# Issuing the loads of an average-pooling kernel from GpSimd's queue instead of SyncE's

## Chip, cores, metric

One core of one Trainium2 chip. The metric is the device time of one execution in microseconds (us), lower is better. A run's span in its profile is about 2 us shorter than its time.

## The reference

A 2x2 average pooling with stride 2 over a float32 tensor of 32x128x256x256. It reads 1074 MB and writes 268 MB; there are three additions and one multiplication for each output element.

```python
def reference(x, kernel_size, stride):          # 2, 2
    ...
    for i in range(h_out):
        for j in range(w_out):
            window = x[:, :, 2*i : 2*i + 2, 2*j : 2*j + 2]   # indices shortened
            output[:, :, i, j] = np.mean(window, axis=(2, 3))
```

## The kernel before

An output row needs two input rows, which lie one after the other in DRAM: 512 floats, 2 KiB, here called a row pair. A full tile holds 32 row pairs in each of 128 partitions. The layout "(p g)" gives each partition 32 row pairs that are adjacent in DRAM, so a load of 8 MiB is 128 pieces of 64 KiB, and a store of 2 MiB is 128 pieces of 16 KiB. There are two input buffers. The last two tiles are split into ten smaller parts, down to one row pair in each partition.

```python
sbuf = ctx.enter_context(tc.tile_pool(name="sbuf", bufs=2))
inv = 1.0 / float(k * k)
r0 = 0
for parts in plan:                       # [32] x 126, then [16, 8, 8], [8, 8, 8, 4, 2, 1, 1]
    in_tile = sbuf.tile([P, G_MAIN, s * w], mybir.dt.float32, name="in_tile")
    g0 = 0
    for g in parts:
        rows = P * g
        xt = xv[r0 : r0 + rows].rearrange("(p g) f -> p g f", p=P)
        ot = ov[r0 : r0 + rows].rearrange("(p g) f -> p g f", p=P)
        # ... r0 += rows
        it = in_tile[:, g0 : g0 + g]
        # ... g0 += g
        nc.sync.dma_start(out=it, in_=xt)                    # load, SyncE's queue
        nc.vector.tensor_add(out=it[:, :, 0:w], ...)         # upper row + lower row
        col_sum = sbuf.tile([P, G_MAIN, w_out], ..., bufs=3)
        nc.vector.tensor_add(out=col_sum[:, :g], ...)        # even columns + odd columns
        nc.scalar.mul(out=col_sum[:, :g], in_=col_sum[:, :g], mul=inv)
        nc.scalar.dma_start(out=ot, in_=col_sum[:, :g])      # store, ScalarE's queue
```

The load of tile i+2 goes into the buffer of tile i, so it may be issued when the second addition of tile i has read that buffer.

Of the kernel before, what the change touches and what calls it, by code (L numbers as in the profile page):

```python
# [1 line left out]

# [4 lines left out]


@with_exitstack  # L10
def kernel(
    ctx: ExitStack,
    tc: tile.TileContext,
    x: bass.AP,
    kernel_size: bass.AP,
    stride: bass.AP,
    out: bass.AP,
):
    nc = tc.nc
    P = nc.NUM_PARTITIONS  # L20

    n, c, h, w = x.shape
    k = int(kernel_size)
    s = int(stride)
    h_out = (h - k) // s + 1
    w_out = (w - k) // s + 1
    R = n * c * h_out

    if k == s and 2 <= k <= 4 and R > 0 and R % P == 0:
        _nonoverlap_pool(ctx, tc, x, out, k, n, c, h, w, h_out, w_out)  # L30
    else:
        _generic_pool(ctx, tc, x, out, k, s, n, c, h, w, h_out, w_out)


def _nonoverlap_pool(ctx, tc, x, out, k, n, c, h, w, h_out, w_out):
    nc = tc.nc
    P = nc.NUM_PARTITIONS
    s = k
    R = n * c * h_out

    hv = h_out * s
    xs = x if hv == h else x[:, :, 0:hv, :]
    xv = xs.rearrange("n c (ho a) w -> (n c ho) (a w)", a=s)
    ov = out.rearrange("n c ho wo -> (n c ho) wo")
    assert xv.shape == (R, s * w) and ov.shape == (R, w_out)

    wu = w_out * s

    unit_bytes = s * w * 4
    G_MAIN = max(1, min(R // P, (64 * 1024) // unit_bytes))  # L50

    total_units = R // P
    nmain, rem_units = divmod(total_units, G_MAIN)
    plan: list[list[int]] = [[G_MAIN] for _ in range(nmain)]
    if rem_units:
        plan.append([rem_units])

    if G_MAIN % 32 == 0 and nmain >= 4 and rem_units == 0:
        u = G_MAIN // 32
        tail = [  # L60
            [16 * u, 8 * u, 8 * u],
            [8 * u, 8 * u, 8 * u, 4 * u, 2 * u, u, u],
        ]
        assert all(sum(t) == G_MAIN for t in tail)
        plan = plan[:-2] + tail
# [6 lines that stand above are left out]
    for parts in plan:  # L72
# [6 lines that stand above are left out]
            r0 += rows  # L79

            it = in_tile[:, g0 : g0 + g]
            g0 += g

            nc.sync.dma_start(out=it, in_=xt)

            for di in range(1, k):
                nc.vector.tensor_add(  # L87
                    out=it[:, :, 0:w],
                    in0=it[:, :, 0:w],
                    in1=it[:, :, di * w : (di + 1) * w],  # L90
                )

            col_sum = sbuf.tile(
                [P, G_MAIN, w_out], mybir.dt.float32, name="col_sum", bufs=3
            )
            nc.vector.tensor_add(  # L96
                out=col_sum[:, :g],
                in0=it[:, :, 0:wu:s],
                in1=it[:, :, 1 : wu + 1 : s],
            )  # L100
            for dj in range(2, k):
                nc.vector.tensor_add(
                    out=col_sum[:, :g],
                    in0=col_sum[:, :g],
                    in1=it[:, :, dj : wu + dj : s],
                )

            nc.scalar.mul(out=col_sum[:, :g], in_=col_sum[:, :g], mul=inv)  # L108

            nc.scalar.dma_start(out=ot, in_=col_sum[:, :g])  # L110
        assert g0 <= G_MAIN

    assert r0 == R, (r0, R)


def _generic_pool(ctx, tc, x, out, k, s, n, c, h, w, h_out, w_out):
    nc = tc.nc
    P = nc.NUM_PARTITIONS

    planes = n * c  # L120
    xp = x.rearrange("n c h w -> (n c) h w")
    op = out.rearrange("n c ho wo -> (n c) ho wo")

    if h_out <= 0 or w_out <= 0 or planes == 0:
        return

    max_in_bytes_per_part = 48 * 1024

    def rows_for(bi):
        return (bi - 1) * s + k  # L130

    BI = 1
    while BI < h_out and rows_for(BI + 1) * w * 4 <= max_in_bytes_per_part:
        BI += 1

    inv = 1.0 / float(k * k)

    pool = ctx.enter_context(tc.tile_pool(name="gen", bufs=2))

    for p0 in range(0, planes, P):  # L140
        pn = min(P, planes - p0)
        for i0 in range(0, h_out, BI):
            bi = min(BI, h_out - i0)
            rows_needed = rows_for(bi)

            in_t = pool.tile([P, rows_for(BI), w], mybir.dt.float32, name="g_in")
            nc.sync.dma_start(
                out=in_t[:pn, :rows_needed, :],
                in_=xp[p0 : p0 + pn, i0 * s : i0 * s + rows_needed, :],
            )  # L150

            acc = pool.tile([P, BI, w_out], mybir.dt.float32, name="g_acc")
            first = True
            for di in range(k):
                for dj in range(k):
                    src = in_t[
                        :pn,
                        di : di + (bi - 1) * s + 1 : s,
                        dj : dj + (w_out - 1) * s + 1 : s,
                    ]  # L160
                    if first:
                        nc.vector.tensor_copy(out=acc[:pn, :bi, :], in_=src)
                        first = False
                    else:
                        nc.vector.tensor_add(
                            out=acc[:pn, :bi, :], in0=acc[:pn, :bi, :], in1=src
                        )

            nc.scalar.mul(out=acc[:pn, :bi, :], in_=acc[:pn, :bi, :], mul=inv)

            nc.scalar.dma_start(
                out=op[p0 : p0 + pn, i0 : i0 + bi, :], in_=acc[:pn, :bi, :]
            )


# [1 line left out]
_INS = ['x', 'kernel_size', 'stride']  # L177
_OUTS = [((32, 128, 128, 128), 'float32')]
#: Inputs that are plain numbers.
_NUMBERS = {'kernel_size': 2, 'stride': 2}  # L180


# [26 lines left out]
```

## Time and profile before

| | before |
|---|---|
| time, median of 2 runs | 3106.58 us (3106.37 to 3106.79) |
| DMA engines' time taken by packets, loads and stores | 79.8% and 20.2% |
| VectorE, ScalarE busy | 54%, 15% |
| one 64 KiB load packet, one 16 KiB store packet | 2.418 us, 0.611 us |
| a full tile's two additions | 8.69 + 4.43 us |

The first lines are from the page of the kernel before: the DMA rows of its 40 slices, and the queue part. A queue's line has its number, its kind, packets, megabytes, and the time its packets took as a share of 16 engines over the span.

```profile
DMA  9999999999999999999999999999999999999999
GB/s 418 436 439 425 436 439 425 436 438 429 433 439 430 431 439 434 427 439 435 426 438 436 427 437 436 428 436 437 427 436 437 428 436 437 429 435 437 432 431 396
...
q1 hardware_dynamic: 19584, 1073.75, 79.8%
q10 hardware_dynamic: 19584, 268.44, 20.2%
```

Queue q1 is the loads', q10 the stores'. Together their packets take 100% of the engines' time: the kernel is bound by the DMA engines, and there is no room in which a faster issue could show.

The view by windows of the kernel before (stretch in us, its length, busy time of each engine, granted clock, DMA share, GB/s) shows where the engines are not full: at the start and in the last 48 us.

```profile
0.00:24.00 24.00, 1.30 (x1) 1.28 (x1) 0.20 (x4) 1.00 0.93 393
24.00:3010.00 2986.00, 1625.35 (x248) 446.62 (x124) 0.00 (x0) 1.00 1.00 434
3010.00:3057.00 47.00, 26.24 (x4) 5.88 (x3) 0.00 (x0) 1.00 0.99 426
3057.00:3105.00 48.00, 28.50 (x20) 11.99 (x11) 0.00 (x0) 1.00 0.89 375
```

A stretch of the timeline of the kernel before (start, duration, engine, line, operation, and in brackets the idle time just before and what ended it). One row of it merges several issues of SyncE's queue:

```profile
1494.01 8.69 DVE L87 TENSOR_TENSOR in_tile<-in_tile 128x8192 f32<-128x8192 f32 x1 [10.97 <-DMA in_tile<-in_x_dram]
1502.79 4.42 DVE L96 TENSOR_TENSOR col_sum<-in_tile 128x4096 f32<-128x4096 f32 x1
1507.24 73.85 SPq L84 DMA_DIRECT2D in_tile<-in_x_dram  x4
1507.25 3.62 ACT L108 ACTIVATE col_sum<-col_sum 128x4096 f32<-128x4096 f32 x1 [20.56 <-DVE col_sum L96]
1510.89 0.34 ACTq L110 DMA_DIRECT2D out_dram<-col_sum  x1
1518.19 8.69 DVE L87 TENSOR_TENSOR in_tile<-in_tile 128x8192 f32<-128x8192 f32 x1 [10.97 <-DMA in_tile<-in_x_dram]
```

VectorE finishes tile i at 1507.21 and then waits 10.97 us for tile i+1 to land. The load of tile i+2 is issued at 1507.24, while tile i+1 is still arriving. Those 11 us are roughly the time by which a load is issued ahead of when the engines run out of loads: the slack.

The issues by size have the median time from issue to landing at the end of the line:

```profile
out_dram<-col_sum ACTq DMA_DIRECT2D x126, 2048.0 KB, 31.6
...
in_tile<-in_x_dram SPq DMA_DIRECT2D x126, 35.1
```

Last, the waits of SyncE's queue in the end of the kernel, from 3010 us on (sum, times, longest):

```profile
SPq L84 <- DVE col_sum L96: 26.4, 2, 13.2
SPq L84 <- DMA in_tile<-in_x_dram: 25.4, 3, 10.6
SPq L84 <- DMA out_dram<-col_sum: 23.7, 4, 15.3
```

Some of the last small loads wait for stores to land, though they share no data. Loads and stores draw their completion semaphores (the counters by which a finished transfer is reported) from one set of eight in this trace, and a load that gets a semaphore whose store is under way has to wait for it.

### The profile page before, as it was taken

The page shows a single profiled execution, that of the slowest core. Times are in us where ns is not written, and L with a number is a line of the kernel's source. Part 1 is how long each engine was busy: PE and PEld are TensorE (multiplying, and loading weights), DVE is VectorE, ACT ScalarE, POOL GpSimd, SP SyncE. Part 2 cuts the span into 40 slices and gives each one's busy share as a digit, 9 for nine tenths or more (in the row PEclk, how much of TensorE's full clock was granted, in tenths as well). Part 3 has the DMA queues.
Part 4 walks back from the last instruction along what each step waited for, and adds up shares of the span by engine and source line. Part 5 has one row for each costly group of instructions (what it writes and reads, how often), then busy time and mean ns, then how long its engine had stood idle before and what let it go on. Part 6 is the DMA issues. An engine that isn't in the chain of part 4 may idle for free. (4 is left out here: it accounts for less than half of the span.)

```text
span 3104.8 us, 1126 instructions
## 1 busy us (share of the span) xinstructions
DVE 1681.4 (54%) x272; ACT 465.8 (15%) x137; POOL 0.2 (0%) x4
## 2 busy tenths in 40 slices
DVE  4555555555555555555555555555555555555556
ACT  1111111111111111111111111111111111111112
POOL 0000000000000000000000000000000000000000
DMA  9999999999999999999999999999999999999999
GB/s 418 436 439 425 436 439 425 436 438 429 433 439 430 431 439 434 427 439 435 426 438 436 427 437 436 428 436 437 427 436 437 428 436 437 429 435 437 432 431 396
DMA packets 39176, 1342.26 MB, mean 432 GB/s; under 512 B 4352, under 2 KB 4736, under 8 KB 5888
## 3 DMA queue, kind: packets, MB, share of 16 engines
q1 hardware_dynamic: 19584, 1073.75, 79.8%
q10 hardware_dynamic: 19584, 268.44, 20.2%
q14 instruction: 8, 0.07, 0.0%
HBM read 1073.74 MB, written 268.44 MB: 432 GB/s over the span
## 5 line engine op out<-in xcount | busy, mean ns | idle before, releaser
L87 DVE TENSOR_TENSOR in_tile<-in_tile 128x8192 f32<-128x8192 f32 (+4 forms) x136 | 1113.9, 8190 | 1406.7 <-DMA in_tile<-in_x_dram 1406.7
L108 ACT ACTIVATE col_sum<-col_sum 128x4096 f32<-128x4096 f32 (+4 forms) x136 | 464.5, 3415 | 2635.9 <-DVE col_sum L96 2635.9
L96 DVE TENSOR_TENSOR col_sum<-in_tile 128x4096 f32<-128x4096 f32 (+4 forms) x136 | 567.8, 4175 | 13.9 <-DMA out_dram<-col_sum 1.8
L108 ACT ACT_TABLE_LOAD x1 | 1.3, 1283 | 0.7 <-PEq L190 0.7
L190 POOL MEMSET const-bfloat16-1.0<- 128x1 bf16 x1 | 0.1, 102 | 0.0
L190 POOL MEMSET const-uint8-127<- 128x1 uint8 x1 | 0.1, 102 | 0.0
L190 POOL MEMSET const-float32-0.0<- 128x1 f32 x1 | 0.1, 99 | 0.2 <-issue 0.2
L190 POOL MEMSET const-float32-1.0<- 128x1 f32 x1 | 0.1, 99 | 0.0
## 6 DMA issues: line engine op xcount, KB each, us to landing
out_dram<-col_sum ACTq DMA_DIRECT2D x126, 2048.0 KB, 31.6
in_tile<-in_x_dram SPq DMA_DIRECT2D x5, 2048.0 KB, 27.5
in_tile<-in_x_dram SPq DMA_DIRECT2D x1, 4096.0 KB, 25.5
out_dram<-col_sum ACTq DMA_DIRECT2D x5, 512.0 KB, 12.0
in_tile<-in_x_dram SPq DMA_DIRECT2D x126, 35.1
out_dram<-col_sum ACTq DMA_DIRECT2D x1, 1024.0 KB, 12.7
in_tile<-in_x_dram SPq DMA_DIRECT2D x1, 1024.0 KB, 16.2
in_tile<-in_x_dram SPq DMA_DIRECT2D x1, 512.0 KB, 16.9
```

The lines of the kernel that those rows point to most:

```text
L87: nc.vector.tensor_add(out=it[:, :, 0:w], in0=it[:, :, 0:w], in1=it[:, :, di * w : (di + 1) * w],)
L96: nc.vector.tensor_add(out=col_sum[:, :g], in0=it[:, :, 0:wu:s], in1=it[:, :, 1 : wu + 1 : s],)
L108: nc.scalar.mul(out=col_sum[:, :g], in_=col_sum[:, :g], mul=inv)
L190: nc = _bacc.Bacc("TRN2", target_bir_lowering=False, num_devices=1)
```

## The change

The loads are issued from GpSimd's queue. Their descriptors, the entries that tell a DMA engine what to move, are then written by software on GpSimd, not by hardware behind SyncE's queue; the profile pages call the two queues software_dynamic and hardware_dynamic. The intent of such a change is to free SyncE's queue, or to keep loads and stores apart.

```diff
-            nc.sync.dma_start(out=it, in_=xt)
+            nc.gpsimd.dma_start(out=it, in_=xt)
```

Stores stay on ScalarE's queue. VectorE's and ScalarE's instructions stay the same and in the same order.

## The prediction

> **What bounds the kernel now.** The 16 DMA engines. The page's slices show DMA at 9 tenths throughout and 432 GB/s; the queue part gives 79.8% of the engines' span to the load queue (q1) and 20.2% to the store queue (q10), together 100%. VectorE is busy 54%, ScalarE 15%. In the steady stage (24 to 3010 us, the view by windows) the DMA share is 1.00 at 434 GB/s. A 64 KiB load packet (one partition's share of an 8 MiB load) takes 2.418 us, a 16 KiB store packet 0.611 us. So loads cost 2479 us and stores 627 us per engine, 3107 us together: the whole span of 3104.8. Only the first 24 us (share 0.93) and the last 48 (0.89) have gaps, about 7 us together.
>
> **What the change does.** 136 load issues move from SyncE's queue to GpSimd's; bytes, tiles, VectorE's and ScalarE's instructions stay. A load now needs its descriptors written by software: the Trainium skill, "DMA: Bandwidth & Descriptors" (Specifications), gives about 1 us to the first byte against 0.6 us from SyncE.
>
> **Is that on the critical path?** Not in the steady stage. Load i+2 is released when the second add of tile i ends, 13.2 us after load i landed (8.69 + 4.43 us); tile i+1 is then still arriving, for the 11 us that VectorE idles before each 128x8192 add. So the next load always queues about 11 us ahead (issue to landing is 35.1 us). A descriptor delay below that is hidden. Exposed is the first load (about 0.5 to 1 us).
>
> The Trainium skill, "SBUF — State Buffer" (DVE blocks DMA), warns that VectorE's two-port operations starve software descriptors. Here all VectorE work is two-input tensor_tensor, which that page puts outside these modes; and the issue falls where VectorE has just finished the tile and idles 11 us. I expect nothing.
>
> A small gain: semaphores of loads and stores are no longer drawn from one set. Before, some of the last small loads waited for stores (SyncE's waits at the end: 23.7 us on stores, 4 times; the chain has a store of 17.8 us ahead of a load of 11.7). Those waits go; but the engines are 0.89 busy there, so at most 2 to 3 us come back.
>
> **Sum.** 3106.6 + 1 (first byte) + 0 to 5 (packets or ring reads slightly slower) - 0 to 3 (tail) = about 3109 us. Range 3098 to 3150. Within 2%: 0.87; slower: 0.12; faster: 0.01.
>
> **What would show it.** After: queue shares again summing to 100% with the loads on a software queue, packet count for loads unchanged at 19584, 64 KiB packets still 2.418 us, steady period unchanged (VectorE idle before the large add about 11 us), issue-to-landing about 35 us, tail without load waits on stores.
>
> **What would make it wrong.** The software generator cutting a 64 KiB row into pieces: from the packet durations measured here, 16 KiB pieces (4 x 0.611 us) would add 26 us, 8 KiB pieces (8 x 0.309) 54 us, 4 KiB pieces (16 x 0.159) 126 us, the only one that passes 2%. The load packets' count would show it. Or: descriptors written so slowly that they exceed the 11 us slack, seen as DMA share below 1.00 in the steady stage; or some DMA engines slowed by reading descriptors from SBUF, seen as a higher 64 KiB packet time at the same count.

## The result

The changed kernel takes 3107.27 us (median of 2 runs, 3107.26 to 3107.27) against 3106.58: ratio 1.0003, interval 0.9984 to 1.0022, the same. The two medians alone give 1.0002.

The page of the changed kernel, the lines that answer to those of before:

```profile
DMA  9999999999999999999999999999999999999999
GB/s 415 439 430 431 439 435 427 439 436 425 438 436 426 437 438 425 436 438 426 436 437 431 432 438 433 428 438 437 426 437 437 427 436 437 428 435 437 428 435 396
...
q0 software_dynamic: 19456, 1073.75, 79.8%
q10 hardware_dynamic: 19584, 268.44, 20.2%
```

The loads are now on q0, written by software, and take the same 79.8%. A 64 KiB packet has the same median of 2.418 us. There are 128 packets fewer. They belong to the last two loads of 256 KB: SyncE's queue shows 256 packets of 2 KiB for them, GpSimd's 128 of 4 KiB; more of that below.

The windows and the timeline of the changed kernel:

```profile
0.00:24.00 24.00, 0.47 (x1) 1.28 (x1) 1.41 (x6) 1.00 0.94 393
24.00:3010.00 2986.00, 1626.20 (x248) 446.01 (x124) 65.73 (x124) 1.00 1.00 433
3010.00:3057.00 47.00, 26.13 (x4) 6.01 (x2) 1.57 (x3) 1.00 1.00 432
3057.00:3105.00 48.00, 28.62 (x21) 12.47 (x11) 3.69 (x7) 1.00 0.91 381
```

```profile
1494.63 8.69 DVE L87 TENSOR_TENSOR in_tile<-in_tile 128x8192 f32<-128x8192 f32 x1 [10.98 <-DMA in_tile<-in_x_dram]
1503.41 4.43 DVE L96 TENSOR_TENSOR col_sum<-in_tile 128x4096 f32<-128x4096 f32 x1
1507.87 3.62 ACT L108 ACTIVATE col_sum<-col_sum 128x4096 f32<-128x4096 f32 x1 [20.57 <-DVE col_sum L96]
1508.13 0.53 POOL L84 DMA_DIRECT2D in_tile<-in_x_dram  x1 [23.66 <-DVE col_sum L96]
1511.52 0.34 ACTq L110 DMA_DIRECT2D out_dram<-col_sum  x1
1518.79 8.69 DVE L87 TENSOR_TENSOR in_tile<-in_tile 128x8192 f32<-128x8192 f32 x1 [10.95 <-DMA in_tile<-in_x_dram]
```

GpSimd starts its issue 0.29 us after the second addition ends (1503.41 + 4.43 = 1507.84, to 1508.13), where SyncE took 0.03 us, and is busy with it for 0.53 us. VectorE goes on 10.95 us after it had finished, when the next tile has landed; before it was 10.97. Nothing of the delay arrives at VectorE.

The issues by size, and GpSimd's waits from 3010 us on:

```profile
in_tile<-in_x_dram POOLq DMA_DIRECT2D x126, 34.8
```

```profile
POOL in_tile L84 <- DVE col_sum L96: 46.3, 2, 23.7
POOL in_tile L84 <- DMA in_tile<-in_x_dram: 3.1, 1, 3.1
```

The waits for stores are gone, as predicted, and nothing was gained by it. VectorE's first addition started 0.83 us later than before (23.53 against 22.70), its last large one 0.62 us later (3043.89 against 3043.27), its last of all 0.60 us later (3102.38 against 3101.78). Between the last large addition and the end the difference hardly moves, so these waits had cost nothing: the loads behind them stood in line for full engines either way. The two last windows show the same few idle microseconds.

One part of the page changes much and means nothing: the chain that ended last. It has 1% on DMA before and 72% after. Before, it was followed back only to 3066.83 us; after, it goes back to the start, presumably because the issues count as GpSimd's instructions and can be followed through. With an equal period this is no finding.

### The profile page after: what moved, and what is told of

Same layout as the page of the kernel before. It is cut to its first block, busy times and chain, and to the rows that moved or that the text cites. A ratio compares the mean times of both kernels' runs of the same rounds, so it can differ in the third digit from the quotient of the medians. Undisturbed runs are those within 1.5% of the kernel's fastest.

```text
span 3105.5 us, 1122 instructions
## 1 busy us (share of the span) xinstructions
DVE 1681.4 (54%) x272; ACT 465.8 (15%) x137; POOL 72.4 (2%) x140
## 3 DMA queue, kind: packets, MB, share of 16 engines
q0 software_dynamic: 19456, 1073.75, 79.8%
q10 hardware_dynamic: 19584, 268.44, 20.2%
## 4 chain that ended last, share of the span: by engine, by line
DMA 72%; DVE 27%; issue 1%; POOL 0%; DVEq 0%; ACT 0%; PEldq 0%
DMA in_tile<-in_x_dram 72%; DVE in_tile L87 18%; DVE col_sum L96 9%; POOL in_tile L84 0%; DVEq L96 0%; DMA out_dram<-col_sum 0%; ACT col_sum L108 0%; PEldq L204 0%
## 5 line engine op out<-in xcount | busy, mean ns | idle before, releaser
L84 POOL DMA_DIRECT2D in_tile<-in_x_dram x136 | 72.2, 531 | 2991.5 <-DVE col_sum L96 2961.4
## 6 DMA issues: line engine op xcount, KB each, us to landing
out_dram<-col_sum ACTq DMA_DIRECT2D x126, 2048.0 KB, 31.6
in_tile<-in_x_dram POOLq DMA_DIRECT2D x126, 34.8
```

The costliest lines, as they stand in the source:

```text
L84: nc.gpsimd.dma_start(out=it, in_=xt)
```

## Experiments

The prediction held. The open question is why: because a slower issue was hidden by the slack (theory A), or because there is no slower issue (rival B)? And do software descriptors cost anything in other conditions? Twelve kernels were run, in three groups, each on one chip with its own runs of the kernel before (medians 3106.34, 3106.40 and 3106.45 us), timed in 3 rounds. All gave the right result but the four without stores. Their outputs are wrong, which doesn't matter for the times.

### 1. Take the slack away: one input buffer

```diff
-        in_tile = sbuf.tile([P, G_MAIN, s * w], mybir.dt.float32, name="in_tile")
+        in_tile = sbuf.tile([P, G_MAIN, s * w], mybir.dt.float32, name="in_tile", bufs=1)
```

> One input buffer instead of two, loads on SyncE as before. The slack is gone: load i+1 starts only after the second add of tile i. Per tile: 19.3 us of load packets (2.418 us x 8 on each engine), up to 4.8 us of the store of the tile before beside it, about 2 us latency, 13.1 us of adds. Both theories: about 35 to 40 us a tile, 4500 to 5100 us in all. This run is the base for onebuf_pool.

> The same with one input buffer, loads on GpSimd. Theory A (software descriptors are slower to start, but two buffers hid it): each of the 128 tiles now shows the extra delay; the first load's start differed by 0.8 us between the two traces (VectorE's first add at 23.53 against 22.70), of which 0.5 us was a later first issue and 0.36 us the time from issue to first packet; so 0.4 to 0.8 us x 127 = 50 to 100 us longer than onebuf_sp. Rival B (the queues are equal apart from start-up): within 10 us of onebuf_sp.

The issues by size of the two kernels, SyncE's first:

```profile
in_tile<-in_x_dram SPq DMA_DIRECT2D x126, 26.4
```

```profile
in_tile<-in_x_dram POOLq DMA_DIRECT2D x126, 28.0
```

onebuf_sp took 5117.40 us (just over the 4500 to 5100 expected) and onebuf_pool 5292.98: 175.6 us more, 1.38 us for each of the 127 loads that wait. Rival B falls: the software issue is slower, and two buffers hide it. But the size is over what theory A said, 50 to 100 us. The packets' times in the two traces divide a tile's path as follows (means of 99 tiles, us):

| | addition's end to issue | issue to first packet | first to last packet | last packet to next addition |
|---|---|---|---|---|
| onebuf_sp | 0.03 | 0.96 | 24.81 | 1.08 |
| onebuf_pool | 0.30 | 1.23 | 25.69 | 1.06 |

The issue is 0.27 us later and the first packet another 0.27 us, 0.54 together, as theory A had it. The other 0.9 us lie within the transfer, where the store of the tile before runs beside the load. Either software descriptors slow a transfer, or load and store mix differently when the load starts half a microsecond later. So the same pair ran without the stores of full tiles:

```diff
-            nc.scalar.dma_start(out=ot, in_=col_sum[:, :g])
+            if g < G_MAIN:
+                nc.scalar.dma_start(out=ot, in_=col_sum[:, :g])
```

> Wrong result on purpose: one input buffer, loads on SyncE, the stores of the full tiles left out, so that no store runs beside a load. Nothing but the load is in the engines: 8 packets x 2.418 = 19.3 us, 2.1 us before and after as in onebuf_sp (0.03 to the issue, 0.96 to the first packet, 1.08 to the add), 13.15 us of adds: about 34.6 us a tile, 4400 to 4500 us. Base for the next run.

> Wrong result on purpose: the same with loads on GpSimd. onebuf_pool was 176 us over onebuf_sp, 1.38 us a tile; by the traces 0.54 us of it lies before the first packet and 0.9 us between first and last packet, where the store of the tile before runs beside the load. Theory S (the 0.9 us come of how load and store mix): without stores only about 0.55 us a tile remain, 60 to 80 us over onebuf_sp_nostore, packets from first to last the same. Rival T (software descriptors slow the transfer itself): 1.4 us a tile remain, about 175 us.

They took 4495.50 and 4566.90 us: 71.4 us apart, 0.56 us a tile. The same division:

| | addition's end to issue | issue to first packet | first to last packet | last packet to next addition |
|---|---|---|---|---|
| onebuf_sp_nostore | 0.03 | 0.96 | 20.55 | 0.44 |
| onebuf_pool_nostore | 0.29 | 1.23 | 20.55 | 0.44 |

The issues by size of these two kernels, SyncE's first; their time to landing counts from an issue that on GpSimd starts later:

```profile
in_tile<-in_x_dram SPq DMA_DIRECT2D x126, 21.8
```

```profile
in_tile<-in_x_dram POOLq DMA_DIRECT2D x126, 22.1
```

The transfer of 8 MiB takes 20.55 us in both. (The expected 19.3 us were 8 packets of 2.418 us; in both traces the sixteen packets of a load that start first, after the engines' pause, last 3.08 us on average and the others 2.42.) Theory S holds and rival T falls: software descriptors don't slow a transfer of 64 KiB pieces; they start it 0.54 us later. The 0.9 us come only with a store beside the load. How the half microsecond's shift makes them was not tried and stays open. The traces show one difference: the store's first packet starts 8.1 us after the load's in onebuf_sp and 5.7 us after it in onebuf_pool, earlier by the time of a whole load packet.

### 2. Measure the slack: delay the issue by a known time

GpSimd overwrites part of the buffer before it issues the load; the load then writes over it. That adds a known time to the way from the addition's end to the issue.

```diff
+            if g == G_MAIN:
+                nc.gpsimd.memset(in_tile[:, 0:8], 0.0)       # delay_long: 0:32
             nc.gpsimd.dma_start(out=it, in_=xt)
```

> The changed kernel, and before each 8 MiB load GpSimd overwrites 8 of the tile's 32 row groups (4096 elements in each partition) with zeros, which the load then overwrites: the issue of the load comes later by that memset (estimated 3 to 8 us). Theory A (11 us of slack ahead of each load): time within 10 us of the changed kernel, VectorE's idle before the large add about 11 us as before, issue to landing shorter by the delay. Rival C (any delay of the issue costs, since the engines drain between loads): 126 x 3 to 8 us = 400 to 1000 us more.

> The same with the whole tile overwritten first (16384 elements in each partition), four times the delay (estimated 12 to 30 us). Theory A: what is over the slack of about 11 us is added to each load, to be read from the trace: period = 24.2 us + (delay + about 2 us of issue and first bytes - 11 us), less what stores fill in. With a memset of 17 us about 8 us x 126 = 1000 us more. If the time is unchanged although the delay is over 15 us, the slack is not what hides it.

delay_short took 3115.54 us. Its timeline, one tile:

```profile
1512.42 4.43 DVE L98 TENSOR_TENSOR col_sum<-in_tile 128x4096 f32<-128x4096 f32 x1
...
1516.91 3.51 POOL L85 MEMSET in_tile<- 128x4096 f32 x1 [19.84 <-DVE col_sum L98]
...
1520.71 0.53 POOL L86 DMA_DIRECT2D in_tile<-in_x_dram  x1 [0.30 <-POOL in_tile L85]
1527.81 8.69 DVE L89 TENSOR_TENSOR in_tile<-in_tile 128x8192 f32<-128x8192 f32 x1 [10.96 <-DMA in_tile<-in_x_dram]
```

The issue comes 3.6 us later (3.51 and the gaps about it), about seven times what the change itself costs, and VectorE's idle before the next large addition is the same 10.96 us. The time from issue to landing falls from 34.8 to 31.2 us, by just the delay. Of the 8.3 us in the span (3113.8 against 3105.5), 6.6 are start-up: the overwriting comes before the first loads too, and VectorE's first wait is 30.1 us instead of 23.5. So the 125 other loads paid 1.7 us in all for 125 delays of 3.6 us.

delay_long took 3400.23 us. The overwriting takes 13.75 us and the issue comes 13.8 us later than in the changed kernel. Its span is 290.5 us longer, 26.9 of them in the first wait (50.4 us). The rest is 264 us, 2.1 us a tile. One tile of its timeline:

```profile
1537.23 13.75 POOL L85 MEMSET in_tile<- 128x16384 f32 x1 [10.68 <-DVE col_sum L98]
...
1550.34 8.69 DVE L89 TENSOR_TENSOR in_tile<-in_tile 128x8192 f32<-128x8192 f32 x1 [13.17 <-DMA in_tile<-in_x_dram]
1551.28 0.53 POOL L86 DMA_DIRECT2D in_tile<-in_x_dram  x1 [0.30 <-POOL in_tile L85]
```

By the slack the loads run out for about 4 us: 0.3 + 13.8 + 1.2 us to the first packet make 15.3 us from the addition's end, and tile i+1 landed 11.0 us after it. In this kernel's trace the gap from a load's last packet to the first of the next is 3.5 us. That a tile is only 2.1 us longer fits what stores fill in: 61% of the stores' packets start while no load packet is under way, and a store landed 13.2 us after its issue, against 31.6. The expectation of 8 us for a memset of 17 had this filling in named but not sized. The slack is real, and a delay past it is paid for. One caution: the DMA share of the steady stage is still 0.98 here, at 398 GB/s instead of 433, since the load packets last longer (64 KiB: 2.62 us on average against 2.42). A busy share near 1 alone doesn't show that the engines lose nothing.

### 3. VectorE beside the writing of descriptors

The Trainium skill, "SBUF — State Buffer" (the box on DVE blocking DMA, and "Who interferes with whom"), says that VectorE's copies in their two-port modes lock GpSimd out and starve software descriptors; it reports a probe in which two-input additions did not stall a transfer, and infers the reason. In the changed kernel the question doesn't arise, since VectorE idles when GpSimd writes. Two kernels make VectorE busy there:

```diff
+            if g == G_MAIN:
+                for _ in range(3):
+                    nc.vector.tensor_copy(out=sb, in_=col_sum[:, 0:16])
+                    # add_beside: tensor_add(out=sb, in0=col_sum[:, 0:16], in1=col_sum[:, 16:32])
             nc.scalar.mul(out=col_sum[:, :g], in_=col_sum[:, :g], mul=inv)
```

> The changed kernel, and VectorE does three fp32 copies of 128x2048 (SBUF to SBUF, results unused) right after the second add of each tile, exactly when GpSimd is released to write the next load's descriptors. If copies of this kind lock GpSimd out of writing descriptors, as the Trainium skill warns, GpSimd's issue instruction should grow from 0.53 us to between 1.5 and 4 us (to the end of one copy or of the three), and the first packet come later; the total stays within 10 us of the changed kernel, since the slack of about 11 us holds it. If they do not, the issue stays at 0.53 us.

> The same with three two-input adds of 128x2048 in the copies' place, about 2.3 us each (measured in the tail of the kernel before), 6.9 us. By the prediction two-input adds do not hinder descriptor writing: issue still 0.53 us, total within 10 us of the changed kernel. If adds hinder it as well, the issue instruction takes 2 to 7 us.

They took 3110.71 and 3111.28 us. First copy_beside's timeline, then add_beside's:

```profile
1508.76 3.75 DVE L113 COPY sb<-col_sum 128x2048 f32<-128x2048 f32 x3
1509.02 1.08 POOL L87 DMA_DIRECT2D in_tile<-in_x_dram  x1 [23.09 <-DVE col_sum L99]
```

```profile
1508.27 6.94 DVE L113 TENSOR_TENSOR sb<-col_sum 128x2048 f32<-128x2048 f32 x3
1508.53 0.53 POOL L87 DMA_DIRECT2D in_tile<-in_x_dram  x1 [23.65 <-DVE col_sum L99]
```

Beside the copies the issue takes 1.08 us instead of 0.53. It ends at 1510.10; the first of the three copies, of 1.23 us, ends at 1509.99. So GpSimd was held to the end of one copy and 0.12 us more (in 115 tiles of the trace alike), which agrees with the page. The expected 1.5 to 4 us took the copies for longer than they are and allowed for all three. Beside additions nothing happens: 0.53 us, as in the page's probe; the reason that the page infers is not tested by this. In both the total stays within 5 us of the changed kernel, and the DMA share of the steady stage is 1.00. So the worst effect of this kind, here half a microsecond a load, would also vanish in the slack.

### 4. Small pieces: does the software generator's packing save time?

In the changed kernel the two smallest loads were packed, two pieces of 2 KiB in one packet of 4 KiB. A 4 KiB packet took 159 ns, two of 2 KiB take 168. If that saving were real, a kernel with small pieces would gain 5% on its loads. The layout "(g p)" makes every load 4096 pieces of 2 KiB and every store 4096 of 512 B:

```diff
-            xt = xv[r0 : r0 + rows].rearrange("(p g) f -> p g f", p=P)
-            ot = ov[r0 : r0 + rows].rearrange("(p g) f -> p g f", p=P)
+            xt = xv[r0 : r0 + rows].rearrange("(g p) f -> p g f", p=P)
+            ot = ov[r0 : r0 + rows].rearrange("(g p) f -> p g f", p=P)
```

> Loads and stores mapped so that each partition's rows lie apart in DRAM: a load is 4096 pieces of 2 KiB instead of 128 of 64 KiB, a store 4096 pieces of 512 B. On SyncE: load packets of 2 KiB at 84 ns, 256 for each engine and load: 21.5 us; store packets at about 27 ns x 256 = 6.9 us; 28.4 us a tile, about 3640 us in all.

> The same layout with the loads on GpSimd. In the changed kernel's trace the two last loads of 128x512 show 64 packets of 4 KiB each where SyncE's queue shows 128 of 2 KiB: the software queue packs pieces. Theory P (it packs always, and a packed packet costs 159 ns where two single ones cost 168): 128 x 0.159 = 20.4 us for the load, 27.3 us a tile, about 3490 us, 4% less than rows_sp. Rival Q (packing is only how the profiler counts, or the pieces are not adjacent in DRAM and so are not packed): same as rows_sp within 1%. Rival R (writing 4096 descriptors takes GpSimd longer than the slack): slower than rows_sp, GpSimd's issue instruction over 11 us.

rows_sp took 3407.96 us and rows_pool 3398.64. Neither total worked out from packet times (3640 and 3490 us) came; the two lie within 1% of each other, as rival Q had it, though the packing is real. The queues of rows_sp, then of rows_pool:

```profile
q1 hardware_dynamic: 526464, 1073.75, 80.9%
q10 hardware_dynamic: 526464, 268.44, 26.0%
```

```profile
q0 software_dynamic: 264320, 1073.75, 77.1%
q10 hardware_dynamic: 526464, 268.44, 27.0%
...
out_dram<-col_sum ACTq DMA_DIRECT2D x126, 2048.0 KB, 57.2
```

Packing is there: half the load packets. But the shares add up to 107% and 104%: packets of small pieces overlap in an engine, so a sum of their durations overstates the time, and the 3640 us worked out from it were 7% too many. The packed kernel is 0.3% faster, but its stores run differently too. Stores now land in 57.2 us (rows_sp: 35.9), and an issue of ScalarE's stores lasts 12.0 us in the median and up to 41.7 (rows_sp: 0.38 and up to 12.1). That fits the Trainium skill, "DMA: Bandwidth & Descriptors" (Queues, rings and completion order), by which an engine changes between queues at packet boundaries, so that larger load packets leave stores a smaller share; no run here isolates it. To see packing without stores, the same pair ran without those of full tiles (the edit is the one of experiment 1):

> Wrong result on purpose: the layout of 2 KiB pieces with two buffers, SyncE, without the stores of full tiles. 256 packets of 84 ns on each engine: 21.5 us a load, about 2760 us, if packets of one queue do not overlap; 20.0 us or less if they overlap as the share of 107% in rows_sp suggests (that was with two queues).

> Wrong result on purpose: the same with loads on GpSimd. Theory P (packing two 2 KiB pieces into one packet saves about 9 ns each time, and in rows_pool the saving was lost to the mixing with stores): 128 packets of 159 ns, 20.4 us a load, about 2620 us, 5% faster than rows_sp_nostore. Rival Q (packing saves no engine time): within 1% of rows_sp_nostore.

They took 2798.29 and 2804.96 us. The windows from 24 to 2750 us, rows_sp_nostore first:

```profile
24.00:2750.00 2726.00, 1651.22 (x252) 452.00 (x125) 0.00 (x0) 1.00 1.05 387
```

```profile
24.00:2750.00 2726.00, 1648.76 (x252) 452.02 (x125) 211.78 (x127) 1.00 1.02 387
```

Both move 387 GB/s in this window and have the same period of 21.68 us a tile (large additions start at 1501.33, 1523.01 and 1544.69 us in the one, at 1503.84, 1525.52 and 1547.21 in the other). Half the packets, the same rate: theory P falls and rival Q's total holds; packing saves no time at this size. (Whether something other than the engines holds both at 387 GB/s, so that a saving couldn't show, was not tested.) The 6.7 us between the two totals lie at the start and in the end parts. The skill's page says the same under "Why small descriptors are slow (HBM only)": packing is worth it only for pieces of at most 256 B. The 159 ns was the duration of a packet in one place, not what it costs in a row: here packed packets had a median of 173 ns and single ones 88, two of them 176. That the 21.5 us a load expected for rows_sp_nostore came out near is luck: 84 ns were assumed and no overlap, but 256 packets of 88 ns make 22.5 us, more than the period, so packets of one queue overlap too. The issue on GpSimd takes 1.68 us for 4096 pieces against 0.53 for 128: more, but far from the slack, so rival R falls too.

No version that beats the kernel before was found. With these queues and this layout an earlier issue has little left to win: the engines are full but for about 7 us at the two ends (by the shares of the windows).

## Why the prediction was right, point by point

- "The 16 DMA engines" bound the kernel, with 3107 us of packets. Right: packet times, shares and period are the same after the change, and so is the time.
- A descriptor delay below about 11 us is hidden. Right, and shown from three sides: with one buffer the slower issue costs 71 to 176 us; a further delay of 3.6 us costs nothing a tile with two buffers; one of 13.8 us costs 2.1 us a tile. No delay between the two was tried, so where the limit lies is not shown; the estimate above puts it nearer 9 us than 11.
- "Exposed is the first load (about 0.5 to 1 us)". Right in size: VectorE's first addition started 0.83 us later, and the end came 0.60 to 0.7 us later. The time to the first byte, the only cost that was named, is less than half of it: from issue to first packet it took 0.36 us longer (1.37 against 1.01), and the first issue itself came 0.51 us later (1.24 against 0.73), which had not been thought of.
- VectorE's additions don't hinder the writing of descriptors. Right; it also didn't matter, since a copy that does hinder it cost 0.55 us of slack and no time in the steady stage.
- The tail gain of "0 to 3" us: nothing came. The waits for stores went, but loads that are issued earlier into full engines land no earlier. This is the same argument as that of the steady stage; the prediction failed to apply it all the way.
- "0 to 5" for slower packets: zero. 64 KiB packets took 2.418 us, and 20.55 us a load alone in the engines on either queue.
- "packet count for loads unchanged at 19584": off by 128. The generator did not cut 64 KiB pieces, which by the prediction's estimate would have cost time, but it packed 2 KiB ones, which had not been thought of; it costs or saves nothing here.

The sum of 3109 us is therefore 1.7 us too high: about 1 us was put on the start, rightly in size, and the terms for packets and tail were both zero. These two had opposite signs and largely cancelled, which is luck and not accuracy.

## What to carry to other kernels

Before moving DMA issues to another queue, ask by how many microseconds an issue runs ahead of when its bytes are needed: the idle time of the consumer that ends with a landing, while the engines stay full, is about that slack, and a delay well within it is free (3.6 us of 11 here). Software descriptors cost about half a microsecond at each start here, which two buffers of 8 MiB hide in the steady stage and one buffer shows at every tile. Waits on an issuing queue, and packet durations summed over overlapping packets, were not time that could be won back here: look whether the engines behind them are full.

## What the Trainium skill lacked or had wrong

- "DMA: Bandwidth & Descriptors" (Specifications) has the first byte at about 1 us with software descriptors and 0.6 with hardware ones. Measured from issue to first packet: 1.23 and 0.96 us. The page leaves out that GpSimd's issue itself starts 0.27 us later after the addition's end (0.30 against 0.03); the whole difference is 0.54 us.
- The same page's table of software-descriptor bandwidth (Bandwidth) has 16 MB in 79.0 us beside 425 GB/s; 16 MB in 79.0 us would be about 212 GB/s. Here 8 MiB took 20.55 us from first to last packet, 408 GB/s (8.39 MB over 20.55 us), so the durations of that table, or what they count, look wrong.
- The same page (SWDGE vs HWDGE vs iDMA) calls packets of at most 4096 B preferred for software descriptors. It doesn't say what becomes of larger pieces: 64 KiB pieces stayed packets of 64 KiB at 2.418 us, and 2 KiB pieces were packed in twos (264,320 load packets instead of 526,464).
- No page says by how much the durations of neighbouring small packets overlap in the profile: 107% of the engines' time with pieces of 2 KiB and 512 B, 100% with 64 and 16 KiB.
- "SBUF — State Buffer" reports of its probe only that two-input additions did not stall the transfer, without a figure: here GpSimd's issue took 0.53 us beside additions, as without them, and 1.08 beside copies.
